# One trunk layer in fp32: the out-gate projection by seven block products, 23 weights split by adding transfers, and the gate's steps chained

## The chip, the cores and the metric

The kernel runs on one core of a Trainium2 chip. The metric is the device time of one execution in microseconds (us), as the median of the runs shown; lower is better. A profile is one execution recorded by the hardware profiler. Five engines work side by side, each with a queue of its own: TensorE (PE: matrix products into PSUM banks of 128 partitions x 512 fp32), VectorE (DVE), ScalarE (ACT), GpSimd (POOL) and SyncE (SP), which here only issues transfers. A transfer issued by POOL can add to what its destination holds; one issued by SP copies.

## The reference: what is computed

Input x is 512 tokens by 1024 channels, one layer, fp32 throughout.

```python
u = rmsnorm(x, norm1_g)
a_glu, q, k, v, r, g_low, gate_a, gate_b = split(u @ w_in)
# branch A: convolution module
c = a_glu[:, :1024] * sigmoid(a_glu[:, 1024:])
c = silu(layernorm(causal_depthwise_conv(c, width 31)))      # over 1024 channels
y_conv = c @ w_conv_out
# branch B: gated linear attention, 4 heads, dk 128, dv 256, chunks of 64
gk = log_sigmoid(g_low @ w_gate_up + b_gate) / 16
o = gla_chunked(q, k, v, gk)
o = rmsnorm_per_head(o) * gla_norm_g * silu(r)               # r: the out-gate, 512 x 1024
y_gla = o @ w_gla_out
h = x + (sigmoid(gate_a) * y_conv + sigmoid(gate_b) * y_gla) @ w_o
u2 = rmsnorm(h, norm2_g)
z = causal_depthwise_conv(u2 @ w_ffn_up, width 3)            # 5632 channels
h = h + (silu(z[:, :2816]) * z[:, 2816:]) @ w_ffn_down
out = rmsnorm(h, final_g)
```

## The kernel before, in words

**Products.** An fp32 product is made of three TensorE products (`mm3`, L294): both operands are split into a high part, rounded to the type TensorE takes at full speed (fp32r), and a low part, what is left. Low x high, high x low and high x high are added up in one PSUM bank. Lines L301, L302 and L303 are the three.

**Weights.** All weights come in blocks of 128 x 1024, in the order of one list, `order` (L149). `load` (L171) issues the transfer of the next block on SP into one of four `raw` buffers; `split_weight` (L229) makes the high part with an ACT copy (L240, L256) and the low part with a DVE subtraction (L241, L259), each into one of four buffers. `weight(name, j)` (L269) gives the block that is due and keeps the splitting two blocks ahead (`LOOK`). It also calls `fill(RATE)`: 5.0 units of waiting side work are taken from `chains` and issued behind the newest low part. The side work is the 31 taps of the width-31 convolution for each of eight channel tiles (`conv_tap`, L600, one DVE instruction each, L607) and, when all these are done, the LayerNorm of branch A in pieces (`norm_chain`, L688). So DVE's side work is spread over TensorE's time by counting weights.

A 128-column tile of a projection (`col_tile`, L305) is eight k-blocks times three products, 24 matmuls of 128x512.

**Stages in order of time.**
1. Start (to 34 us): x is loaded, transposed by TensorE and normalised; the order of the work is written out by hand. `spread_gain` (L382) turns the transposed token tiles 2 and 3 into high (L389, ACT) and low parts (L391, DVE) in pieces of 128x128; the first half of v is projected at the same time (L529).
2. `w_glu`: 16 column tiles, two for each channel tile of branch A; the sigmoid on ACT, the product on DVE (L615), then the 31 taps are put into `chains`.
3. `w_low`, the low-rank decay; its three steps Abs, Exp and Ln over four heads (`gate`, L724) are put on ACT in one piece, with the first block of the second half of v behind it (`values(1, gate)`, L742).
4. Heads (`Head`, L763; loop L884): for head h, TensorE projects q and k, then two column tiles of w_r (`gate_r`, L871: the tile of r and a Silu on ACT, L876), and the scores, states and outputs of head h − 1 are laid between them. `outputs` (L843) normalises with a root made on POOL (`rsqrt`, L347, L349) and multiplies on ACT (L859); `gated` (L861) transposes back on TensorE (L865), multiplies with gain and gate on DVE (L868) and splits.
5. `w_gb` and `w_gla` mixed (L880 to L916), with sigmoid(gate_b); then `w_ga` (L918) with its sigmoids. Meanwhile the LayerNorm runs as side work: mean on TensorE (L652), centred tiles (L655), squares (L657, L662), variance (L637), root, spread over the partitions (L644), and for each channel tile a product (L674), Silu (L676) and split (L684, L685).
6. `w_conv` with the merge, then w_o and, in three groups, the channel mixer with `w_up` and `w_down`.

**Seven block products.** `w_o` and `w_down` are already computed by a scheme in which a product of 2 x 2 blocks takes seven block products, not eight (`seven`, L958). The operands are the blocks named in `STEPS` (L48): a11 and a12 and a22 as they are, and s1, n2, s4 and n3 sums of blocks. The sums of weights are made in memory: a block is loaded into a `kept` tile, and a POOL transfer that adds brings the next one (L210, L227); DVE adds once (L220). A `block` (L185) takes one row of the weight's layout, which holds two k-blocks by 512 columns.

ACT can hold one set of function tables at a time; going from one set to another shows as a line ACT_TABLE_LOAD.

Of the kernel before, what the change touches and what calls it, by code (L numbers as in the profile page):

```python
# [17 lines left out]
P = 128  # L18
# [18 lines left out]
RATE = 5.0  # L37
WARM = 7
# [4 lines left out]
SEVEN = {"w_o": KT // 2, "w_down": FT // 2}  # L43
# [3 lines left out]
STEPS += [(step, d) for step in ("n2", "s4", "n3", "a22") for d in (0, 1)]  # L47
# [3 lines left out]

C_A, C_G, C_Q, C_K, C_V, C_R = 0, 1024, 2048, 2560, 3072, 4096
# [15 lines left out]
def trunk_layer(ctx: ExitStack, tc: tile.TileContext, a: dict, out: bass.AP):  # L68
# [16 lines left out]
    ps = pool("psum", 1, bass.MemoryType.PSUM)  # L85
    edge = ctx.enter_context(tc.tile_pool(name="edge", bufs=1, side="right"))
    heap_scope, hp = scoped("heap", 26)
    conv_scope, vp = scoped("conv", 10)
    gla_scope, gp = scoped("gla", 1, "right")

# [61 lines left out]
    order += [("w_v", KT // 2 + j) for j in range(KT // 2)]  # L152
    for h in range(HEADS):
        order += [("w_qk", 2 * h), ("w_qk", 2 * h + 1), ("w_r", 2 * h), ("w_r", 2 * h + 1)]
    order += [("w_gb", m) for m in range(AHEAD)]
    for m in range(KT):
        order += [("w_gla", m)] + [("w_gb", m + AHEAD)] * (m + AHEAD < KT)
# [25 lines left out]
    def block(name, pairs, d, row, col):  # L183

        pairs = pairs[2 * d : 2 * d + 2]  # L185
        first = pairs[0][row]
        w = a[name][col * SEVEN[name] + first // 2]
        return w if len(pairs) == 2 else w[:, row * T : (row + 1) * T]

    def keep_tile(name):  # L190
        if name == "w_o":
            return tp.tile([P, D], F32, tag="x", name=nm("kept"), bufs=3)
        return fp.tile([P, D], F32, tag="kept", name=nm("kept"), bufs=2)
# [3 lines left out]
    def load_block(name, pairs, step, d):  # L197
# [11 lines left out]
        if step == "n3":  # L209
            nc.gpsimd.dma_start(dst, block(name, pairs, d, 1, 1), accum_op=ALU.add)  # L210
# [4 lines left out]
    def operand(raw, pairs, step, d):  # L215
# [3 lines left out]
        if step == "n2":  # L219
# [3 lines left out]
    def sum_on(name, pairs, step, d):  # L223

        if step in ("a11", "n2"):
            nxt = block(name, pairs, d, *((0, 1) if step == "a11" else (1, 0)))
            nc.gpsimd.dma_start(kept[pairs, d], nxt, accum_op=ALU.add)  # L227

    def split_weight(between=None):  # L229
        if len(ready) < len(order):  # L230
# [4 lines left out]
            if name in SEVEN:  # L235
                raw = operand(raw, *spec)
# [4 lines left out]
                nc.vector.tensor_tensor(lo, raw, hi.bitcast(F32), ALU.subtract)  # L241
# [14 lines left out]
            nc.scalar.copy(hi, raw)  # L256
            if between:
# [10 lines left out]
    def weight(name, j, ahead=LOOK):  # L268
# [4 lines left out]
        fill(RATE)  # L273
# [215 lines left out]

    def renormed(t):  # L490
# [3 lines left out]
        for g in range(2):  # L494
            f = unscaled[t, g]
            nc.vector.tensor_tensor(by_token(f), by_token(f), rb, ALU.mult)
        for g in range(2):
            f = unscaled[t, g]
            split_by(by_token(f), *(u1[g][i][:, :, t * P : (t + 1) * P] for i in range(2)))
# [43 lines left out]
    here = lambda t: (lambda g, k: tuple(u1[g][i][:, k, t * P : (t + 1) * P] for i in range(2)))  # L543
# [25 lines left out]
    spread_gain(banks[2], 0, here(2))  # L569
# [5 lines left out]
    spread_gain(banks[3], 0, here(3))  # L575
# [13 lines left out]
    def values(n, middle):  # L589
        row_half("w_v", n * KT // 2, n, acts1, KT, v_done, n == 1, middle)  # L590

# [4 lines left out]

    conv = [None] * KT

# [9 lines left out]

    for k in range(KT):
        pg = col_tile(weight("w_glu", 2 * k + 1), acts1)  # L610
# [6 lines left out]
            [(1 if tap < CW - 1 else 0, lambda k=k, tap=tap, c=c: conv_tap(k, tap, c)) for tap in reversed(range(CW))]  # L617
        )


    ca = [None] * KT
    stat = {}

    def add_up(tiles, key):
        def first():
            stat[key] = btmp()
            nc.vector.tensor_tensor(stat[key], tiles(0), tiles(1), ALU.add)

        def more(k):
            nc.vector.tensor_tensor(stat[key], stat[key], tiles(k), ALU.add)  # L630

        return [first] + [lambda k=k: more(k) for k in range(2, KT)]
# [91 lines left out]
    def gate(step):  # L724
        if step > 0:
            return
        with tc.manual_schedule(engines={ET.Activation}):
            for h in range(HEADS):
# [4 lines left out]
                nc.scalar.activation(ab[h], pg, AF.Abs, bias=bg)  # L733
                ls.append(heap())
                nc.vector.tensor_scalar(ls[h], pg, bg, 0.0, ALU.add, ALU.min)
            for h in range(HEADS):
                nc.scalar.activation(ab[h], ab[h], AF.Exp, scale=-1.0)
            for h in range(HEADS):
                nc.scalar.activation(ab[h], ab[h], AF.Ln, bias=1.0)
                nc.vector.tensor_tensor(ls[h], ls[h], ab[h], ALU.subtract)  # L740

    values(1, gate)  # L742


# [17 lines left out]
    class Head:  # L762
# [11 lines left out]
        def decays(self):  # L774
# [8 lines left out]
            nc.scalar.activation(self.end, self.end, AF.Exp, scale=G16)  # L783
# [56 lines left out]
        def outputs(self):  # L840
            self.o = tp.tile([P, NT, DV], F32, tag="x", name=nm("o"), bufs=3)
            for g in range(2):
# [14 lines left out]
                for i in range(2):  # L857
                    o = self.o[:, 2 * g + i, :]
                    nc.scalar.activation(o, po[:, i * DV : (i + 1) * DV], AF.Copy, scale=r[:, i : i + 1])  # L859

        def gated(self):  # L861
            for s in range(2):
# [3 lines left out]
                f = tmp()  # L866
                m = 2 * self.h + s
                nc.vector.scalar_tensor_tensor(f, po, pp[:, PP_GG + s : PP_GG + s + 1], sr[m], ALU.mult, ALU.mult)  # L868
                oa[m] = split(f)

    sr = [None] * KT  # L871

    def gate_r(m):
# [4 lines left out]
    gbs = {}  # L878

    def gate_b(m):  # L880
        gbs[m] = col_tile(weight("w_gb", m), acts1)


# [419 lines left out]
```

## Time and profile before

| | |
|---|---|
| Time, median of 3 runs | 838.59 us (837.83 to 838.66) |
| The profiled execution | 838.75 us |
| Its span, first to last instruction | 837.0 us |
| Granted TensorE clock, mean | 0.997 |
| PE busy | 827.7 us, 99% of the span |
| PE's weight loads (beside the matmuls) | 691.3 us, 83% |
| DVE busy | 648.8 us, 78% |
| ACT busy | 400.0 us, 48% |
| POOL busy | 41.7 us, 5% |
| Bytes moved | 97.27 MB, 116 GB/s on average |

Busy shares are means over stages with different limits. A stage is read from the windows, which give each engine's busy time in a stretch, and from the waits, which say what TensorE stood still for and how long. In the chain of work that ended last, each piece is followed back to what released it; a piece is given with its start, its length and the line. In timelines, "x8" at the end of a row joins eight like instructions, and a bracket gives the idle time ahead of the row and who ended it. The mean duration of one matmul overlaps with that of the next, so the price of a matmul is taken from a row of many.

### The profile page before, as it was taken

What the parts mean: (1) busy time and instruction counts of PE and PEld (TensorE: products, weight loads), DVE (VectorE), ACT (ScalarE), POOL (GpSimd) and SP (SyncE); (2) the same over time, 40 slices, a digit from 0 to 9 for tenths busy, and PEclk for the clock granted to TensorE, in tenths of its full rate; (3) what the DMA queues carried; (4) which work ended last, traced back from release to release, by engine and by line L of the source; (5) the groups of instructions that cost most, each with busy time, mean ns of one, the idle gap of its engine ahead of it and who ended that gap; (6) DMA issues with size and microseconds to landing.
All of it is one profiled execution on the core that took longest, in us unless ns stands there. A gap on an engine that the chain in (4) does not pass through costs nothing.

```text
span 837.0 us, 10108 instructions
## 1 busy us (share of the span) xinstructions
PE 827.7 (99%) x3841; PEld 691.3 (83%) x3841; DVE 648.8 (78%) x952; ACT 400.0 (48%) x598; POOL 41.7 (5%) x64
## 2 busy tenths in 40 slices
PE   9999999999999999999999999999999999999996
PEld 7888888888888888888888898888888888888885
DVE  5789879999998798744687758778757787667795
ACT  7732337435443422449444765444434444444454
POOL 1000000000100100000001000001000010000111
PEclk9999999999999999999999999999999999999998
DMA  8332222222222322222347643234742249222462
GB/s 299 115 101 101 100 92 93 93 85 84 93 76 76 126 100 94 83 99 78 106 96 197 181 152 131 97 95 108 213 151 87 66 89 286 101 82 96 101 125 101
DMA packets 28465, 97.27 MB, mean 116 GB/s; under 512 B 3232, under 2 KB 3504, under 8 KB 28416
## 3 DMA queue, kind: packets, MB, share of 16 engines
q1 hardware_dynamic: 24784, 84.62, 29.8%
q0 software_dynamic: 3456, 11.80, 8.3%
q8 instruction: 30, 0.49, 0.2%
q10 hardware_dynamic: 176, 0.20, 0.1%
q14 instruction: 19, 0.16, 0.1%
HBM read 94.51 MB, written 2.10 MB: 115 GB/s over the span
## 4 chain that ended last, share of the span: by engine, by line
PE 90%; issue 3%; DVE 2%; DMA 2%; ACT 2%; POOL 0%; SPq 0%; POOLq 0%; ACTq 0%; DVEq 0%
PE mm L301 27%; PE mm L303 27%; PE mm L302 27%; PE mm L529 3%; DMA raw<-in_w_down_dram 1%; PE ax L848 1%; DVE hres L998 1%; DMA x<-in_x_dram 1%; PE ax L850 1%; PE ax L830 1%; PE ax L301 1%; PE ax L303 1%; PE ax L302 1%; PE ax L380 1%; ACT whi L240 0%
## 5 line engine op out<-in xcount | busy, mean ns | idle before, releaser
L301 PE MATMUL mm<-uh,wlo 128*128 128x512 f32 (+1 forms) x768 | 294.7, 384 | 0.0
L303 PE MATMUL mm<-uh,whi 128*128 128x512 f32 (+1 forms) x768 | 292.2, 380 | 0.0
L302 PE MATMUL mm<-ul,whi 128*128 128x512 f32 (+1 forms) x768 | 292.0, 380 | 0.0
L256 ACT CAST whi<-raw 128x1024 fp32r<-128x1024 f32 x116 | 120.9, 1047 | 126.3 <-PE mm L303 94.8
L259 DVE TENSOR_TENSOR wlo<-raw,whi 128x1024 fp32r<-128x1024 f32 x116 | 141.1, 1220 | 35.0 <-ACT whi L256 34.8
L303 PEld LDWEIGHTS mm<-uh,whi 128*128 128x128 f32 x768 | 144.4, 188 | 27.9
L302 PEld LDWEIGHTS mm<-ul,whi 128*128 128x128 f32 x768 | 144.5, 188 | 27.2
L301 PEld LDWEIGHTS mm<-uh,wlo 128*128 128x128 f32 x768 | 144.5, 188 | 27.0
L607 DVE SCALAR_TENSOR_TENSOR c<-h,pp,c 128x511 f32<-128x511 f32 (+14 forms) x240 | 162.6, 732 | 0.7
L1078 DVE SCALAR_TENSOR_TENSOR tmp<-mm,pp,tmp 128x511 f32<-128x511 f32 x88 | 65.8, 748 | 66.7 <-ACT tmp L1076 65.5
L1076 ACT ACTIVATE tmp<-mm,pp 128x512 f32<-128x512 f32 x44 | 34.3, 779 | 61.5 <-PE mm L303 61.5
L240 ACT CAST whi<-kept 128x1024 fp32r<-128x1024 f32 (+1 forms) x32 | 31.7, 994 | 25.1 <-DVE kept L220 11.3
L241 DVE TENSOR_TENSOR wlo<-kept,whi 128x1024 fp32r<-128x1024 f32 (+1 forms) x32 | 36.7, 1153 | 4.3 <-ACT whi L240 4.1
L998 DVE TENSOR_TENSOR hres<-hres,mm 128x512 f32<-128x512 f32 (+1 forms) x49 | 32.6, 671 | 6.1 <-PE mm L303 3.7
L240 ACT CAST whi<-raw 128x1024 fp32r<-128x1024 f32 (+1 forms) x24 | 23.7, 995 | 18.0 <-PE mm L303 16.8
L241 DVE TENSOR_TENSOR wlo<-raw,whi 128x1024 fp32r<-128x1024 f32 (+1 forms) x24 | 27.3, 1153 | 1.9 <-ACT whi L240 1.8
L302 PE MATMUL mm<-wlo,sh 128*128 128x512 f32 x66 | 25.8, 391 | 0.0
L303 PE MATMUL mm<-whi,sh 128*128 128x512 f32 x66 | 25.7, 389 | 0.0
L301 PE MATMUL mm<-whi,sl 128*128 128x512 f32 x66 | 25.5, 389 | 0.0
L301 PE MATMUL mm<-h,wlo 128*128 128x512 f32 x64 | 25.4, 397 | 0.0
L349 POOL TENSOR_TENSOR rstd<-var,mhalf 128x1 f32<-128x1 f32 (+1 forms) x16 | 13.3, 839 | 239.9 <-DVE var L855 196.6
L303 PE MATMUL mm<-h,whi 128*128 128x512 f32 x64 | 24.9, 390 | 0.0
(258 smaller groups left out, 1146.6 us busy)
## 6 DMA issues: line engine op xcount, KB each, us to landing
raw<-in_w_up_dram SPq DMA_DIRECT2D x44, 512.0 KB, 3.5
raw<-in_w_glu_dram SPq DMA_DIRECT2D x16, 512.0 KB, 3.3
raw<-in_w_down_dram SPq DMA_DIRECT2D x15, 512.0 KB, 3.3
kept<-in_w_down_dram POOLq DMA_DIRECT2D x10, 512.0 KB, 5.5
raw<-in_w_v_dram SPq DMA_DIRECT2D x8, 512.0 KB, 3.9
raw<-in_w_qk_dram SPq DMA_DIRECT2D x8, 512.0 KB, 3.2
raw<-in_w_r_dram SPq DMA_DIRECT2D x8, 512.0 KB, 3.3
raw<-in_w_gb_dram SPq DMA_DIRECT2D x8, 512.0 KB, 3.2
```

Source lines behind the costliest of these rows:

```text
L240: nc.scalar.copy(hi, raw)
L241: nc.vector.tensor_tensor(lo, raw, hi.bitcast(F32), ALU.subtract)
L256: nc.scalar.copy(hi, raw)
L259: pace[0] = nc.vector.tensor_tensor(lo, raw, hi.bitcast(F32), ALU.subtract)
L301: nc.tensor.matmul(acc, ll, rh, start=first, stop=False, **kw)
L302: nc.tensor.matmul(acc, lh, rl, start=False, stop=False, **kw)
L303: nc.tensor.matmul(acc, lh, rh, start=False, stop=last, **kw)
L529: nc.tensor.matmul(accs[t], src(k)[a_low], w, start=first, stop=last)
L607: nc.vector.scalar_tensor_tensor(y[:, s:], c[:, : T - s], w, y[:, s:], ALU.mult, ALU.add)
L998: nc.vector.tensor_tensor(hres[t, n][:, c], hres[t, n][:, c], x[:, c], op)
L1076: nc.scalar.activation(z, acc, AF.Identity, bias=pp[:, PP_FB + m : PP_FB + m + 1], scale=w[2])
L1078: nc.vector.scalar_tensor_tensor(z[:, s:], acc[:, : T - s], w[j], z[:, s:], ALU.mult, ALU.add)
```

## The change

**w_r by seven products.** r = u @ w_r moves out of the head loop. A `unit` computes it in the seven-product scheme, straight after the decay projection, with 14 weight blocks of 12 matmuls (`R_STEPS`). Its result lies by token instead of by channel: eight tiles `sr[t, n]` of 128 tokens x 512 columns. For this:
- w_r is laid out anew in DRAM, by 16 transfers on SP (`lay_rows`, two before each channel tile of w_glu), each 256 KB in pieces of 512 bytes, into eight tiles `rows_r`.
- All sums of w_r's blocks are made by adding transfers on POOL (eight of them); DVE adds none.
- The sums of activations (s1, n2, s4, n3) are formed on DVE and split on ACT and DVE, as a chain of side work. They need the activations as whole fp32 tiles, so the start keeps them (`whole`): for token tiles 2 and 3 `gained_normed` multiplies a 128x512 tile on DVE, then splits it with an ACT copy and a DVE subtraction, in place of `spread_gain`.

**23 low parts by transfers.** For the blocks in `ADDED` (seven of w_glu, all eight of w_gb and of w_gla) the low part is no longer subtracted on DVE: ACT writes the block's negative, rounded like the high part, and a POOL transfer adds the block once more from DRAM.

**Rates.** `fill` gets a rate of its own for each weight (`RATES`); the sums for the LayerNorm's mean are put into the chains of taps; the pauses in `norm_chain` are changed.

**Gate steps and Silus.** Abs, Exp and Ln are laid at three places of the r unit, and each ACT instruction is issued behind the one before (`behind`). The eight Silus of r run together, in place, after the decays of head 0. ACT_TABLE_LOAD goes from 22 to 13.

**Heads.** The places of w_r's tiles are taken by the second half of v (heads 0 and 1) and by w_gb's first four tiles (heads 2 and 3); the other four follow, then all of w_gla. The output's norm factor and the gate are multiplied in one DVE instruction (128x256) in place of ACT's; the gain is applied on the way back from the transposes, where ACT makes the high part and DVE the low.

The diff, cut to its core:

```diff
+RATES = {"w_glu": 6.2, "w_r": 0.3, "w_low": 0.0, "w_v": 5.0, "w_qk": 4.2, "w_gb": 6.0, "w_gla": 6.5, "w_ga": 9.0}
+ADDED = {("w_glu", 2 * k) for k in range(1, KT)} | {(name, m) for name in ("w_gb", "w_gla") for m in range(KT)}
-SEVEN = {"w_o": KT // 2, "w_down": FT // 2}
+SEVEN = {"w_o": KT // 2, "w_down": FT // 2, "w_r": KT // 2}
+R_STEPS = [("a11", 0), ("a11", 1), ("a12", 0), ("s1", 0), ("s1", 1), ("a12", 1)] + LATE
+GATE_AT = [("a11", 1), ("a12", 0), ("n2", 1)]
+    def lay_rows(j):
+        n, k = j // 4, j % 4 * 2
+        for i in range(2):
+            src = a["w_r"][n * 4 : n * 4 + 4, :, (k + i) * P : (k + i + 1) * P]
+            dst = rows_r[j][:, i * T : (i + 1) * T]
+            nc.sync.dma_start(dst.rearrange("p (c x) -> p c x", x=P), src.rearrange("c p x -> p c x"))
...
-    order += [("w_v", KT // 2 + j) for j in range(KT // 2)]
+    order += [("w_r", (O_PAIRS, step, d)) for step, d in R_STEPS]
...
+            if order[len(ready)] in ADDED:
+                nc.scalar.activation(lo, raw, AF.Copy, scale=-1.0)
+                nc.gpsimd.dma_start(lo, a[name][spec], accum_op=ALU.add)
+                ready.append((hi, lo))
+                load()
+                return
...
-        fill(RATE)
+        fill(RATES.get(name, RATE))
...
+    def gained_normed(t):
+        for g in range(2):
+            gain = gains[:, g * 4 : g * 4 + 4].unsqueeze(2).to_broadcast([P, 4, P])
+            nc.vector.tensor_tensor(into_whole(t, g)[0], by_token(banks[t][g]), gain, ALU.mult)
+        for g in range(2):
+            f, parts = into_whole(t, g)
+            split_by(f, *parts)
...
-    spread_gain(banks[2], 0, here(2))
+    gained_normed(2)
...
+    def sums_chain():
+        chain = []
+        for g in range(2):
+            chain += [(1, lambda n=n, g=g: form(n, g)) for n in ("s1", "n2", "s4", "n3")]
+        for n in ("s1", "n2", "s4", "n3"):
+            chain += [(1, lambda n=n, g=g: place(n, g)) for g in range(2)]
+        return chain
...
     for k in range(KT):
+        lay_rows(k)
         pg = col_tile(weight("w_glu", 2 * k + 1), acts1)
...
-        chain = [(1, f) for f in add_up(lambda k: conv[k], "sum")]
-        chain[-1] = (RATE, chain[-1][1])
-        chain.append((0, ln_mean))
+        chain = [(8, lambda: None), (0, ln_mean)]
         chain.extend((2, lambda k=k: ln_center(k)) for k in range(KT))
-        chain[-1] = (RATE, chain[-1][1])
-        chain.append((RATE, ln_var))
+        chain[-1] = (13, chain[-1][1])
+        chain.append((13, ln_var))
...
+    def behind(emit):
+        if last_act[0] is None:
+            last_act[0] = emit()
+            return
+        with tc.issue_after(last_act[0].ins):
+            last_act[0] = emit()
...
+        while steps:                       # unit("w_r", ...)
+            step, d = steps.pop(0)
+            parts = [(d, weight(name, (O_PAIRS, step, d)))]
...
+                        mm3(acc, (ah, al), (w[0][:, c], w[1][:, c]), opens and d == 0 and j == 0, last, not opens)
+                if parts[-1][0] == 1:
+                    at(step, i)
+                    sink(step, i, acc)
...
-                    nc.scalar.activation(o, po[:, i * DV : (i + 1) * DV], AF.Copy, scale=r[:, i : i + 1])
+                    nc.vector.scalar_tensor_tensor(self.o[:, t, :], half, r[:, i : i + 1], gate, ALU.mult, ALU.mult)
...
-                nc.vector.scalar_tensor_tensor(f, po, pp[:, PP_GG + s : PP_GG + s + 1], sr[m], ALU.mult, ALU.mult)
-                oa[m] = split(f)
+                nc.scalar.activation(hi, po, AF.Copy, scale=gain)
+                nc.vector.scalar_tensor_tensor(lo, po, gain, hi.bitcast(F32), ALU.mult, ALU.subtract)
...
-        pr = col_tile(weight("w_r", m), acts1)
-        sr[m] = heap()
-        nc.scalar.activation(sr[m], pr, AF.Silu)
+            if h == 0:
+                for y in sr.values():
+                    behind(lambda: nc.scalar.activation(y, y, AF.Silu))
```

More of the change, by code (lines that the diff above doesn't have):

```diff
@@ L541, in v_done @@
             nc.scalar.activation(vt[t, n], acc, AF.Copy, scale=r)
-    here = lambda t: (lambda g, k: tuple(u1[g][i][:, k, t * P : (t + 1) * P] for i in range(2)))
+    for half in range(2):
+        for g in range(2):
+            whole[half, g] = sum_tile()
     banks[1] = [ax_bank(), mm_bank()]
@@ L574, in trunk_layer @@
     r1[1] = rms(1)
-    spread_gain(banks[3], 0, here(3))
+    gained_normed(3)
     renormed(0)
@@ L617, in trunk_layer @@
             [(1 if tap < CW - 1 else 0, lambda k=k, tap=tap, c=c: conv_tap(k, tap, c)) for tap in reversed(range(CW))]
+            + [(1 if k else 0, lambda k=k: add_up(k))]
         )
     ca = [None] * KT
[L622 to L632, printed above, removed]
     def token_sums(s):
```

207 lines of the change are left out of this document (158 added, 49 removed).

## The prediction

> **What bounds the kernel now.** I read the page first (engine shares, then the engine shares of the chain that ended last), then the waits of TensorE, then the stages one by one.
>
> ```profile
> span 837.0 us, 10108 instructions
> PE 827.7 (99%) x3841; PEld 691.3 (83%) x3841; DVE 648.8 (78%) x952; ACT 400.0 (48%) x598; POOL 41.7 (5%) x64
> ...
> PE 90%; issue 3%; DVE 2%; DMA 2%; ACT 2%; POOL 0%; SPq 0%; POOLq 0%; ACTq 0%; DVEq 0%
> ```
>
> The waits of TensorE (us in total, times, longest), and one piece of the chain (start, us, what):
>
> ```profile
> PE ax L441 <- DVE ones L408: 1.1, 1, 1.1
> PE ax L380 <- DMA x<-in_x_dram: 0.7, 1, 0.7
> PE ax L380 <- ACT un L400: 0.3, 1, 0.3
> ...
> 28.74 5.49 PE mm L529 x24
> ```
>
> Stages (stretch, its length, busy time of PE, weight load, DVE, ACT and POOL, granted clock, DMA share, GB/s), the GLU projections, the heads, w_gla, w_ga and the output projection w_o:
>
> ```profile
> 34.00:121.40 87.40, 87.40 (x388) 72.35 (x387) 71.61 (x99) 28.48 (x35) 0.53 (x1) 1.00 0.35 117
> ...
> 147.00:276.00 129.00, 129.00 (x625) 108.76 (x624) 123.58 (x199) 57.12 (x95) 5.77 (x6) 1.00 0.26 86
> ...
> 293.00:358.00 65.00, 65.00 (x287) 53.45 (x286) 53.85 (x74) 19.73 (x26) 0.00 (x0) 1.00 0.29 97
> 358.00:401.00 43.00, 43.00 (x199) 35.84 (x198) 18.43 (x24) 32.73 (x40) 1.01 (x1) 1.00 0.24 80
> ...
> 444.00:490.00 46.00, 45.72 (x241) 38.87 (x240) 35.36 (x58) 30.03 (x58) 5.73 (x7) 1.00 0.72 213
> ```
>
> TensorE works in 99% of the span, and the chain is 90% TensorE. The three wait rows are all that the profile charges to it: 2.1 us. In each stage TensorE is full. So time falls only where matmuls go, and the other engines count only where they make TensorE wait. The narrow place is the heads: DVE 123.58 of 129 us. The profiled execution took 838.75 us, 0.16 above the median of 838.59; the sum is made against 838.75.
>
> **Matmuls removed.** Eight column tiles of 24 matmuls (192) become 14 weight blocks of 12 (168). The chain row prices 24 full matmuls at 5.49 us: **−5.5 us**. Every other matmul of the changed program is there in the same number. As TensorE had almost no waits to lose, this is also the most that can be won; all else can only take back.
>
> **Start.** For token tiles 2 and 3 the normalised activations were made in eight short pairs, ACT then DVE. Now DVE multiplies whole 512-wide tiles, ACT copies, DVE subtracts.
>
> ```profile
> 20.94 2.16 DVE L391 SCALAR_TENSOR_TENSOR ul<-ax,gains,uh 128x128 fp32r<-128x128 f32 x8 [0.32 <-ACT uh L389]
> ...
> 22.54 0.48 PE L529 MATMUL mm<-whi,ul 128*128 128x512 f32 x1
> ...
> 24.36 2.16 DVE L391 SCALAR_TENSOR_TENSOR ul<-ax,gains,uh 128x128 fp32r<-128x128 f32 x8 [0.87 <-ACT uh L389]
> ...
> 25.51 0.47 PE L529 MATMUL mm<-whi,ul 128*128 128x512 f32 x1
> ...
> 27.15 1.22 ACT L469 CAST uh<-h 128x512 fp32r<-128x512 f32 x2 [1.79 <-DVE h L496]
> ...
> 27.81 1.29 DVE L470 TENSOR_TENSOR ul<-h,uh 128x512 fp32r<-128x512 f32 x2
> ```
>
> The pairs gave a first low part soon after 20.94, and TensorE took it at 22.54. In the new form, from about 20.6: multiply 0.65, copy 0.61, subtract 0.65 (half of the last two rows) puts the first at 22.5 to 22.7, so a stall of up to 0.2. For tile 3, whose banks are read once DVE is done with tile 2 (about 23.4), two multiplies, the copy behind the first and a subtract end near 26.1, against 25.51: 0.6. I take **+0.8**, bounds 0 and 1.5 (all six steps of a tile in series, less the slack seen).
>
> **GLU stage.** Rate 6.2 in place of 5.0 means 2.4 more convolution taps per pair of weights; seven low parts leave DVE.
>
> ```profile
> L256 ACT CAST whi<-raw 128x1024 fp32r<-128x1024 f32 x116 | 120.9, 1047 | 126.3 <-PE mm L303 94.8
> L259 DVE TENSOR_TENSOR wlo<-raw,whi 128x1024 fp32r<-128x1024 f32 x116 | 141.1, 1220 | 35.0 <-ACT whi L256 34.8
> ...
> L607 DVE SCALAR_TENSOR_TENSOR c<-h,pp,c 128x511 f32<-128x511 f32 (+14 forms) x240 | 162.6, 732 | 0.7
> ...
> L227 POOL DMA_DIRECT2D kept<-in_w_down_dram x12: 849/862/878, 560.9 to 808.6; - x12
> ...
> DMA to landing us min/median/max: 3.9/5.5/9.2
> ...
> q1 hardware_dynamic: 24784, 84.62, 29.8%
> q0 software_dynamic: 3456, 11.80, 8.3%
> ```
>
> DVE per pair (11.0 us of TensorE): 12.4 taps at 0.73, one low part 1.22, one product 0.69, in all 11.0; two neighbours overlap a little (1.29 for two of 0.69, the last row of the fence before), so it is some 10.2: full, not over. Taps that come late delay nobody here. **0**, up to +1.
>
> **The 23 adding transfers.** Each replaces a 1.22 us subtraction by an ACT copy of the negative (1.05), a POOL issue (0.86) and a landing of 3.9 to 9.2 us: 7.4 median, 11.1 worst. A low part's buffer is free once the weight four places earlier is used, so three weights of 5.49 us (16.5) lie between. Covered, **0**. If the cover went (an ACT or POOL queue late by over 5 us), each late one would cost what is over. With the r unit's eight sums POOL issues 31 more, 27 us in all; they stand ahead of the small powers of the norms, at 0.86 us each.
>
> **Re-laying w_r.** 16 transfers of 256 KB, DRAM to DRAM in 512-byte pieces, go on SP, the queue of the weight loads; eight issue back to back ahead of one of the GLU loads. No row shows this kind. From the queue rows: SP moves 84.62 MB in 29.8% of 837 us, 339 GB/s, so 0.8 us a transfer if bytes set the price, 1.5 us at the adding queue's 170 GB/s, and, if a piece costs what a packet does (29.8% × 837 × 16 engines / 24784 = 161 ns), 512 × 161 / 16 = 5.2 us, 41 us for eight. SP may run about 15 us for eight of them before the load behind is late (three weights less one landing of 3 us): 60 ns a piece. I take the bytes' price, by the row of SP's own queue, which is the nearest: **0**; upper end +25. DRAM to DRAM both reads and writes; twice 0.8 is still under the 60 ns a piece (1.9 us).
>
> **The r unit.** 38 us of TensorE, like w_o, whose window shows 45.72 of 46 busy with the same steps. On the path: sums of weights that land by adding transfers.
>
> ```profile
> kept<-in_w_o_dram POOLq DMA_DIRECT2D x4, 512.0 KB, 7.0
> ```
>
> Ten loads at 1.29 us (161 ns × 128 / 16) and eight adds at 2.58 (8.3% × 837 × 16 / 3456 = 322 ns) are 33.5 us of 38: 88% DMA, more than w_o's 72%. The second s1 sum is needed some 5.5 us after its add can start; the add took 5.5 elsewhere and 7.0 in w_o. The 28 us of DVE (14 low parts, 16 sums and splits, sinks) fit. The chained gate steps wait on one another on ACT, with copies of weights behind them, but 27 us of ACT fit in 38. **+0.5**; bounds 0 and 3.7 (9.2 − 5.5).
>
> **Heads.** The gate multiply moves into the normalisation, on DVE. Two groups of the heads' window (count, then busy us, mean ns, then idle before):
>
> ```profile
> L868 DVE SCALAR_TENSOR_TENSOR tmp<-ax,pp,h 128x512 f32<-128x512 f32 x6 | 4.2, 746 | 1.5 <-PE ax L865 1.5
> ...
> L837 DVE SCALAR_TENSOR_TENSOR state<-state,dec,ax 128x256 f32<-128x256 f32 x8 | 3.8, 476 | 0.0
> ```
>
> Per head DVE gains four 128x256 products (4 × 0.476 = 1.9) and changes two products and two subtractions (2 × 0.746 + 2 × 0.69) for two products (1.5): +0.5. Taps go from 20 to 18.4 in heads 0 and 1 (−1.2) and to 20.4 in heads 2 and 3 (+0.3), where two low parts go too (−2.4). DVE so ends at 27.4 and 26.5 us of a 29.3 us head, against 28.1 before. But its products now lie between the norm and the transposes that TensorE is to do next, and four late value banks (then four gb banks) hold four of five `mm` banks. **+0.2**; bounds 0 and 2 (0.5 a head).
>
> **w_gla, w_ga, LayerNorm.** w_gla loses eight subtractions in a stage where DVE has 11 us to spare. The LayerNorm is set closer:
>
> ```profile
> 341.06 0.86 PE ax L652 x2
> ...
> 357.26 0.69 DVE L662 TENSOR_TENSOR btmp<-btmp,btmp 128x512 f32<-128x512 f32 x1 [0.76 <-ACT btmp L657]
> ...
> 363.72 0.79 PE ax L637 x8
> ...
> 370.11 0.89 PE ax L644 x8
> ...
> 371.81 1.28 ACT L676 ACT_TABLE_LOAD   x1
> 373.10 1.52 ACT L676 ACTIVATE btmp<-c,pp 128x512 f32<-128x512 f32 x2
> ```
>
> Between mean (341.06) and variance (363.72) lie four weights now, three (16.5 us) after; the squares were done 16.9 after the mean, so up to 0.6 is lost, less as some DVE work between them is gone. From the spread (370.11) to the convolution's projection lay 28 us; now 16.5, and the first two column tiles are interleaved, so that the last normalised tile is wanted some 9.5 us later: 26. ACT's work there, eight Silus, eight copies, four table loads and the weights' copies, is some 21 to 25 us. **+0.3**; bounds 0 and 1.5. Table loads go from 22 to 13 (−11.5 us of ACT), mostly where ACT has idle time: 0.
>
> **Sum:** 838.75 − 5.5 + 0.8 + 0.5 + 0.2 + 0.3 = 835.05, or **834.9** as a median.
>
> **Rivals.**
> *A, no change.* The sums of the r unit or the heads' norm come late at several of these steps: 3.7 (r) with 1.5 (start) and the LayerNorm's 0.6 gives 5.8 back: about 838.5. For it: DMA 88%, adds at 7.0. Against: w_o lost 0.28.
> *B, slower: the re-laying starves the weight loads.* It decides from about 85 ns a piece (8 × 512 × 85 / 16 = 21.8 us, some 7 more than the cover); at 100 ns the loss is 10.6 and the time 845.5. For it: eight in a row ahead of a load, and 161 ns for a packet of 3.4 KB. Against: 512-byte pieces carry a seventh of those bytes.
> *C, slower: DVE in the heads.* DVE was at 96%; if its new products wait on the norm's power behind POOL issues, each head loses 2 us or so: 8 us, 843. Against: 0.7 to 1.6 us a head freed.
> *D, table loads cost more than their row.* With an extra stop of 1.4 us at each of the four loads of the LayerNorm's last part, that chain grows by 5.5 to some 29 of its 26: about +4, 839. Against it: the row at 371.81 ends at 373.09 and the next instruction starts at 373.10.
>
> The Trainium skill (ScalarE: Activation LUTs, What ACT_TABLE_LOAD costs) has that stop: 1283 ns of load and about 1380 ns of drain, 2.66 us a switch. This trace shows the load and no drain, so D gets little.
>
> **Chances.** Forecast 0.60 (832.9 to 836.9); A 0.14; B 0.12; C 0.09; D 0.03; 0.02 is left for more gain than the sum. The measurement tells apart 0.2%, 1.7 us: same is 836.9 to 840.3. Faster 0.62; same 0.15 (A with part of D); slower 0.23. The range leaves out little below 833 (nothing but −5.5 pays) and half of B above: 833.0 to 843.0; the forecast's own is 833.0 to 836.9.
>
> **What would show it.** TensorE with 24 fewer 128x512 matmuls and 819 to 823 us busy; waits in the start on the tile split of under 1.5 us; in the r unit waits on weights under 2 us together; no wait on a GLU weight while the re-laying runs; heads of 29.3 us with DVE under 96%; the convolution's projection not waiting over 1 us. The forecast is wrong if a `w_glu` load lands late behind the re-laying, if adds in the r unit land after 9 us, or if a head is longer than 30 us.

## The result

The changed kernel takes 835.61 us (median of 7 runs, 834.5 to 836.71), the kernel before 838.41 in the same session (7 runs, 837.83 to 838.66). The ratio is 0.9967, with a 95% interval of 0.9955 to 0.9978: 2.8 us faster. Forecast were 834.9 us and a range of 833.0 to 843.0. In two further sessions the same kernel had medians of 835.46 and 835.46, at ratios of 0.9959 (0.9948 to 0.9971) and 0.9965 (0.9952 to 0.9977).

The page of the changed kernel, its first two lines, and three of the wait rows of TensorE (us in total, times, longest):

```profile
span 834.2 us, 10185 instructions
...
PE 823.8 (99%) x3817; PEld 686.7 (82%) x3817; DVE 645.3 (77%) x957; ACT 415.9 (50%) x606; POOL 69.6 (8%) x95
```

```profile
PE ax L411 <- DVE ul L422: 1.2, 1, 1.2
...
PE ax L332 <- DVE h L818: 0.6, 1, 0.6
...
PE mm L581 <- DVE ul L501: 0.2, 1, 0.2
```

TensorE has 24 instructions fewer, and the span is 2.8 us shorter (837.0 before). 24 matmuls are 5.45 us at the 0.227 us from one start to the next that both traces have, so part of it came back. The three rows name the largest pieces: 0.2 in the start, 0.6 in the r unit, and 1.2 in the norm behind w_o, a stage that the change doesn't touch. A row counts idle time alone. All that TensorE lost is got by taking each distance from one start to the next over the median of its kind, adding these up, and taking off the same sum of the trace of before: 0.6 us in the start, 0.8 in the r unit, 0.2 to 0.3 in the heads, 0.3 in the LayerNorm and 1.3 in w_o's stage. As x landed 0.1 us earlier, this makes 3.15 us in all.

That is 0.5 us more than the spans leave room for. The rest lies behind the last matmul, from the issue of the last SP transfer of the output (before, then changed) to the end of the span:

```profile
832.59 0.33 SPq L1160 DMA_DIRECT2D out_dram<-y  x1
```

```profile
830.29 0.33 SPq L1322 DMA_DIRECT2D out_dram<-y  x1
```

It took 4.4 us before (to 837.0) and 3.9 after (to 834.2). Outside the span it is the other way: time less span is 2.0 us in the changed kernel's runs and 1.7 in those of before, so that 0.2 us of the shorter end reach the time. With these the profiled execution adds up: 838.75 − 5.45 + 3.15 − 0.2 = 836.25, and it took 836.23. Why the end differs isn't shown.

The stages of the changed kernel (length, busy time of PE, weight load, DVE, ACT, POOL, clock, DMA share, GB/s): GLU, r unit, heads with the rest of w_gb's first tiles, w_o.

```profile
34.00:121.90 87.90, 87.90 (x390) 72.78 (x389) 79.78 (x118) 39.08 (x51) 7.66 (x9) 1.00 0.63 165
...
125.40:163.50 38.10, 37.55 (x166) 30.73 (x165) 29.15 (x34) 27.52 (x37) 5.27 (x7) 1.00 0.79 192
163.50:293.00 129.50, 129.50 (x627) 109.19 (x626) 122.09 (x208) 61.32 (x97) 15.48 (x16) 1.00 0.48 122
...
441.00:487.00 46.00, 44.54 (x232) 37.73 (x231) 34.89 (x57) 29.45 (x56) 5.73 (x7) 1.00 0.72 208
```

TensorE is full in the GLU stage and in the heads, where DVE is at 91% and 94%. It loses 0.55 us in the r unit and 1.46 in w_o's stage.

**The start.** The first matmul that takes token tile 3, and DVE ahead of it:

```profile
25.98 0.50 PE L581 MATMUL mm<-whi,ul 128*128 128x512 f32 x1 [0.17 <-DVE ul L501]
```

```profile
23.78 0.16 DVE L488 SCALAR_TENSOR_TENSOR var<-ss 128x1 f32<-128x1 f32 x1 [0.68 <-ACT junk L486]
23.86 1.28 DVE L548 TENSOR_TENSOR f<-ax,gains 128x512 f32<-128x512 f32 x2
25.23 1.29 DVE L501 TENSOR_TENSOR ul<-f,uh 128x512 fp32r<-128x512 f32 x2
```

It starts at 25.98, 0.47 later than before. DVE stood 0.68 us for the sum of a norm that ACT had not squared yet (L488), and only then made tile 3's products.

**The r unit.** Five rows, of ACT, DVE and TensorE, in the order in which each stands behind the one above:

```profile
130.09 1.05 ACT L265 CAST whi<-kept 128x1024 fp32r<-128x1024 f32 x1 [1.37 <-DMA kept<-rows]
131.04 1.04 ACT L265 CAST whi<-raw 128x1024 fp32r<-128x1024 f32 x1
```

```profile
132.96 1.22 DVE L266 TENSOR_TENSOR wlo<-raw,whi 128x1024 fp32r<-128x1024 f32 x1
134.21 2.07 DVE L818 TENSOR_SCALAR h<-ax,pp 128x512 f32<-128x512 f32 x3
```

```profile
135.02 0.50 PE L332 MATMUL ax<-whi,ul 128*128 128x512 f32 x1 [0.55 <-DVE h L818]
```

ACT waits 1.37 us for an adding transfer (which took 5.4 us to land, no more than such a transfer mostly does), DVE makes low parts behind ACT, the gate's minimum (L818) stands behind these low parts, and its PSUM bank is the one that the step a12 wants.

**w_o.** Part of the chain of work that ended last (start, us, what):

```profile
453.42 0.60 POOL kept L252
454.02 13.53 DMA kept<-in_w_o_dram
...
467.65 1.06 ACT whi L265
...
468.74 1.23 DVE wlo L266
469.96 0.08 DVE var L1203
```

One adding transfer of w_o took 13.5 us to land; the slowest of the kernel before was 9.2. The norm's variance (L1203) stands on DVE behind the low part of that sum, and TensorE's transposes (L411) wait for what is made from it.

**Re-laying and adding.** The two lines of the re-laying transfers, and the landing times of the 23 adding ones:

```profile
L99 SPq DMA_DIRECT2D rows<-in_w_r_dram x16: 552/677/2523, 7.9 to 28.1; - x16
...
DMA to landing us min/median/max: 4.4/6.3/8.0
```

```profile
DMA to landing us min/median/max: 5.3/6.9/10.0
```

All 16 were issued between 7.9 and 28.1 us. Eight of them stand back to back ahead of a GLU load:

```profile
20.07 8.76 SPq L99 DMA_DIRECT2D rows<-in_w_r_dram  x8
33.43 4.16 SPq L191 DMA_DIRECT2D raw<-in_w_glu_dram  x4
```

They are issued by 28.8 us, and that load goes out at 33.43, where the kernel before issued it at 33.19. No wait of TensorE is charged to either kind.

### The profile page after: what moved, and what is told of

The parts are those of the page before. It is cut to its first block, busy times and chain, and to the rows that moved or that the text cites. A ratio compares the mean times of both kernels' runs of the same rounds, so it can differ in the third digit from the quotient of the medians.

```text
span 834.2 us, 10185 instructions
## 1 busy us (share of the span) xinstructions
PE 823.8 (99%) x3817; PEld 686.7 (82%) x3817; DVE 645.3 (77%) x957; ACT 415.9 (50%) x606; POOL 69.6 (8%) x95
## 4 chain that ended last, share of the span: by engine, by line
PE 86%; DMA 4%; issue 4%; ACT 2%; DVE 2%; POOL 1%; SPq 0%; POOLq 0%; ACTq 0%; DVEq 0%
PE mm L332 26%; PE mm L333 26%; PE mm L334 26%; DMA kept<-in_w_o_dram 2%; PE mm L581 1%; PE ax L332 1%; PE ax L999 1%; PE ax L333 1%; PE ax L334 1%; DMA x<-in_x_dram 1%; DMA kept<-rows 1%; DMA raw<-in_w_o_dram 1%; PE ax L1001 1%; PE ax L981 1%; DMA hres<-in_x_dram 1%
## 5 line engine op out<-in xcount | busy, mean ns | idle before, releaser
L332 PE MATMUL mm<-uh,wlo 128*128 128x512 f32 (+1 forms) x704 | 269.8, 383 | 0.0
L334 PE MATMUL mm<-uh,whi 128*128 128x512 f32 (+1 forms) x704 | 267.3, 380 | 0.0
L333 PE MATMUL mm<-ul,whi 128*128 128x512 f32 (+1 forms) x704 | 267.1, 379 | 0.0
L688 DVE SCALAR_TENSOR_TENSOR c<-h,pp,c 128x507 f32<-128x507 f32 (+21 forms) x240 | 162.3, 732 | 1.2 <-ACT c L685 0.6
L333 PEld LDWEIGHTS mm<-ul,whi 128*128 128x128 f32 x704 | 132.5, 188 | 25.0 <-ACT h L1082 0.2
L332 PEld LDWEIGHTS mm<-uh,wlo 128*128 128x128 f32 x704 | 132.5, 188 | 24.9 <-issue 0.2
L334 PEld LDWEIGHTS mm<-uh,whi 128*128 128x128 f32 x704 | 132.4, 188 | 25.0
L290 DVE TENSOR_TENSOR wlo<-raw,whi 128x1024 fp32r<-128x1024 f32 x85 | 103.2, 1220 | 14.7 <-ACT whi L281 14.4
L283 ACT ACTIVATE wlo<-raw 128x1024 fp32r<-128x1024 f32 x23 | 24.4, 1061 | 74.0 <-PE mm L332 68.5
L252 POOL DMA_DIRECT2D kept<-in_w_down_dram x12 | 10.3, 859 | 271.8 <-DVE wlo L266 271.8
```

Source lines behind the costliest of these rows:

```text
L283: nc.scalar.activation(lo, raw, AF.Copy, scale=-1.0)
L290: pace[0] = nc.vector.tensor_tensor(lo, raw, hi.bitcast(F32), ALU.subtract)
L332: nc.tensor.matmul(acc, ll, rh, start=first, stop=False, **kw)
L333: nc.tensor.matmul(acc, lh, rl, start=False, stop=False, **kw)
L334: nc.tensor.matmul(acc, lh, rh, start=False, stop=last, **kw)
L688: nc.vector.scalar_tensor_tensor(y[:, s:], c[:, : T - s], w, y[:, s:], ALU.mult, ALU.add)
```

## Experiments

Each ratio is to the kernel before in the same session, since that had medians from 838.4 to 840.5 in the several sessions. In the session of experiments 1 to 4 it took 840.49, and the changed kernel as it is was not run there. The ratios of these four don't stand beside its 0.9959 to 0.9967, and the waits in the traces decide. All but one are edits of the changed kernel.

**1. Leave out 24 matmuls.**

```diff
-                for d, w in parts:
+                for d, w in parts if step != "a22" else ():
```

> The changed kernel without the 24 matmuls of the r unit's last step (a22); its weights are still loaded and split. It leaves out one of the seven block products, so part of r is missing. Theory (TensorE sets the pace of the r unit, and 24 matmuls are worth 24 x 0.227 = 5.45 us wherever they are taken): 835.6 - 5.5 = 830.1, between 829 and 831.5, and the stretch of the r unit 32.7 us long in place of 38.1. Rival (the adding transfers or DVE set the pace there, so that the sums come late once the matmuls are shorter): less than 3 us gained, 832.6 or more, with waits of TensorE on weights behind the unit.

831.38 us against 840.49 before: 0.9892 (0.9878 to 0.9907). Experiments 3 and 4 took 834.8 and 834.9 us in the same session, so some 3.5 us more; the span is 828.4 us against 833.3 in experiment 5's first profile, 4.9 us less. The r unit's stretch:

```profile
125.40:158.10 32.70, 32.30 (x142) 26.39 (x141) 24.50 (x28) 25.28 (x34) 5.25 (x6) 1.00 0.86 209
```

```profile
PE mm L332 <- DVE q L945: 0.7, 1, 0.7
```

TensorE is busy for 32.30 of 32.70 us with DMA at 86%; a new wait of 0.7 us comes in the first head. The theory holds: the time lies in its range, TensorE sets the pace of the unit, and by the spans 24 matmuls are worth their 5.45 us less the new wait. What the change lost was not lost by a unit bound by its sums.

**2. Subtract again, with no adding transfers for the 23 weights.**

```diff
-ADDED = {("w_glu", 2 * k) for k in range(1, KT)} | {(name, m) for name in ("w_gb", "w_gla") for m in range(KT)}
+ADDED = set()
```

> The changed kernel with all 23 low parts made by DVE subtractions again, no adding transfer for them; rates and all else as changed. Theory (the adding transfers pay for the higher rates): DVE gets 7 x 1.14 = 8.0 us more in the GLU stage, 79.8 + 8.0 = 87.8 of 87.9 us, and 8 x 1.14 = 9.1 us more from the heads to the end of w_gb, 122.1 + 9.1 = 131.2 of 129.5 us: over-full, so TensorE waits there for low parts, 2 to 5 us in all, 837.5 to 840.5. Rival (DVE has slack enough, since its order can let taps slip): the same time as the changed kernel, 835.6 within 0.8.

836.14 us, 0.9948 (0.9931 to 0.9965). The theory fell, since the waits that it named are absent; the rival's figure came. It is still 1.3 us above experiments 3 and 4 of the same session.

```profile
34.00:121.90 87.90, 87.90 (x389) 72.86 (x388) 86.33 (x124) 33.26 (x43) 0.53 (x1) 1.00 0.34 122
...
163.50:293.00 129.50, 129.50 (x628) 109.36 (x627) 120.90 (x198) 52.48 (x87) 7.15 (x6) 1.00 0.24 85
```

```profile
PE ax L332 <- DVE h L818: 1.1, 1, 1.1
```

DVE is at 98% in the GLU stage and TensorE still never waits there. The heads have not more DVE work but less (120.90): side work slips to later stages, where there is room. The adding transfers save DVE 25 us (670.1 us busy without them, 645.3 with) and TensorE, by this profile, only part of the 1.1 us at the gate: in the r unit it lost 2.4 us here, against 0.8 in the changed kernel's first profile.

**3. The swap in the start.**

```diff
-    r1[1] = rms(1)
     gained_normed(3)
+    r1[1] = rms(1)
```

> The changed kernel with one swap in the start: the products and splits of token tile 3 are put ahead of the norm of tile 1 (its two squares on ACT, its sum on DVE). Theory (the stall of 0.47 us at 25.5 us comes of tile 3's first low part, which stands on DVE behind that sum): the first matmul of tile 3 starts at 25.5 in place of 25.98 and 0.3 to 0.5 us go: 835.2. Rival (the two products, the copy and the subtraction alone are too long): the stall stays at 0.3 or more, 835.6. Rival (the norm of tile 1 now comes late for the next tile): a new stall near 28.9.

834.82 us, 0.9933 (0.9919 to 0.9948).

```profile
23.13 1.28 DVE L548 TENSOR_TENSOR f<-ax,gains 128x512 f32<-128x512 f32 x2
24.50 1.29 DVE L501 TENSOR_TENSOR ul<-f,uh 128x512 fp32r<-128x512 f32 x2
```

The products start at 23.13, and no wait on L501 is left; the next tile isn't late. The profile settles it, since 0.4 us is less than the spread of the times. The theory holds: not the longer chain itself but its place on DVE, behind the norm of another tile, made the stall.

**4. PSUM banks changed over.**

```diff
-bank[of[step], i] = ax_bank() if step == "a12" else mm_bank()
+bank[of[step], i] = ax_bank() if step == "s1" else mm_bank()
```

> The changed kernel with the PSUM banks of two steps of the r unit changed over: a12 takes banks of the kind mm, s1 takes banks of the kind ax. Theory (TensorE's wait of 0.6 us at 134.1 is for the banks of the gate's products, which DVE reads late): the wait goes, 0.5 to 0.8 us less, 834.9, and no wait is charged to the gate's minimum on DVE. Rival (the wait is moved on to the step s1, or was hidden by another): 835.6.

834.86 us, 0.9935 (0.992 to 0.9949), but the wait is there:

```profile
PE ax L332 <- DVE h L818: 0.4, 1, 0.4
```

It has moved to the step s1, which now wants these banks. That was the first rival; the time alone would have spoken for the theory.

**5. The changed kernel again, twice.**

> The changed kernel as it is, so that it stands beside the other runs on one chip. Theory (the stall of 1.2 us at 475 us in its first profile, behind an adding transfer of w_o that took 13.5 us to land, is one execution's and no part of the change): that wait is absent, or under 0.3 us, and the span is 833 to 833.5. Rival (the change has moved the transfers of w_o's stage, which it does not touch, so that the add lands late as a rule): the wait at 470 to 476 us is there again with 1 us or more.

835.46 us (835.41 to 835.65), span 833.3 us. No wait in w_o's norm beyond that of the kernel before: the theory held for the wait. But an add of w_o took 12.1 us to land here too, so the slow landing is not one execution's. In place of that wait another shows in the r unit, with the chain behind it:

```profile
132.31 9.97 DMA kept<-rows
...
142.38 1.06 ACT whi L265
...
143.46 1.24 DVE wlo L266
...
144.74 0.50 PE mm L333
```

The add of a weight sum (POOL, on `kept`) took 9.97 us, and TensorE waits for the low part behind it, 0.3 us.

> The changed kernel as it is, once more beside the version with both small moves. Theory: 835 to 836 us, and of the waits of TensorE those at 25.5 us (0.3 to 0.4), at 134 us (0.3 to 0.7) and at 144 us (0.1 to 0.4) are there again, the one at 475 us, seen in one of the earlier profiles with 1.2 us, not or small.

835.46 us (834.16 to 836.69). The profiled execution was the shortest of the five, 834.16. The stall in the start is there again with 0.4 us and that at 134 us with 0.4, those at 144 and 475 us are not: in the r unit TensorE lost 0.5 us in all, and in w_o's stage no more than in the kernel before.

**6. The swap and an earlier gate.**

```diff
-    r1[1] = rms(1)
     gained_normed(3)
+    r1[1] = rms(1)
...
-GATE_AT = [("a11", 1), ("a12", 0), ("n2", 1)]
+GATE_AT = [("a11", 0), ("a12", 0), ("n2", 1)]
```

> The swap in the start (tile 3's products ahead of tile 1's norm) and the gate's first step one place earlier in the r unit (after the first of the two a11 tiles). Theory (what holds TensorE at 134 us is a chain: the adding transfer for the first s1 sum lands late, ACT waits for it, the low part on DVE waits for ACT, the gate's minimum stands behind that on DVE, and its bank is wanted by a12): the gate's products now come 2.7 us earlier, but the minimum still stands behind the same low part on DVE, so 0.2 to 0.6 us stay at 131 to 135 us; the start's 0.4 us go. Against the changed kernel in the same call: 0.3 to 0.9 us less. Rival (an earlier gate is enough): no wait over 0.1 us left there. Rival (the low-rank product isn't split yet at the earlier place): a new wait of 0.3 us or more at 128 us.

834.45 us (6 runs) against the changed kernel's 835.46 in the same session: 1.0 less, at 0.9954 (0.9941 to 0.9967). One of its runs took 837.28.

```profile
128.63 2.07 DVE L818 TENSOR_SCALAR h<-ax,pp 128x512 f32<-128x512 f32 x3
```

```profile
PE ax L813 <- DVE h L797: 0.2, 1, 0.2
```

The gate's minimum now runs at 128.63, ahead of the late low part, not behind it as expected, and the wait at 134 is gone: the first rival. The second came too: 0.4 us ahead of 127.4 until the low-rank product is split.

> The version with tile 3's products ahead of tile 1's norm and the gate's first step one place earlier, once more, since one of its six times was 2.5 us above the others. Theory: 0.8 to 1.2 us under the changed kernel in the same call, the sum of the waits that its first profile did not show. Rival (its gain was the chance of one profile): within 0.3 us of the changed kernel.

834.73 us (834.02 to 837.89) against 835.46: 0.7 less, between the theory's 0.8 and the rival's 0.3; 0.9957 (0.9944 to 0.9969). The profile fell on the longest run, 837.89, and shows what that is made of:

```profile
PE ax L411 <- DVE ul L422: 2.0, 1, 2.0
...
PE mm L333 <- DVE wlo L266: 0.8, 1, 0.8
```

Both are waits behind adding transfers, in w_o's norm and in the r unit, the first of them on the same path as the 1.2 us of the first profile. Against this version's first profile (834.17) the two stages lost 2.8 us more, of 3.8 us between the spans. The version was shorter by its median in both sessions, but the intervals overlap, so its gain over the changed kernel is not proved by times.

**7. The adding transfers alone, in the kernel before.** (The same two lines as in the change, put into the kernel before; the rate stays 5.0.)

> The kernel before with one part of the change alone: the 23 low parts made by ACT and adding transfers, with the old rate and everything else as it was. Theory (DVE is off the path, so relief for it buys nothing by itself, and the adding transfers are covered by 16 us of lead): ratio to before 1.000, between 0.9985 and 1.0015, with DVE 23 x 1.14 = 26 us less busy. Rival (the landings of 7 to 10 us make weights late): waits of TensorE on weights, 1 us or more slower. Rival (DVE at 96% in the heads cost something that no wait row shows): 1 us or more faster.

839.0 us against 838.69: 1.0005 (0.9997 to 1.0014).

```profile
PE 828.3 (99%) x3841; PEld 691.4 (83%) x3841; DVE 620.9 (74%) x929; ACT 421.2 (50%) x621; POOL 62.1 (7%) x87
```

DVE is 27.9 us less busy (648.8 before) and the time is the same. The theory holds, both ways: no weight came late, and relief for an engine off the path bought nothing. The one new wait of TensorE, 0.3 us at 291.5, is for a product of the last head, not for a weight.

**8. Lay w_r out twice.**

```diff
         lay_rows(k)
+        lay_rows(k, more_r)
```

> The changed kernel with w_r laid out twice, into a second set of DRAM tiles that nothing reads: 16 more transfers of 256 KB in pieces of 512 bytes on SP. Theory (a piece costs 27 ns, 0.86 us of all 16 engines for a transfer, and they run in the start behind x and the first weights, with slack): 13.8 us more of transfers move the time by 0 to 1 us. Rival (the start is at the limit of the DMA engines, 80 to 90% busy up to 40 us, so that the first GLU weights come late): 3 us or more, with TensorE waiting on weights between 30 and 60 us.

834.8 us, 0.9954 (0.9942 to 0.9967).

```profile
L100 SPq DMA_DIRECT2D rows<-in_w_r_dram x16: 552/692/1691, 7.5 to 50.2; - x16
L100 SPq DMA_DIRECT2D more<-in_w_r_dram x16: 557/694/4927, 10.0 to 55.9; - x16
```

The 32 transfers reach into the GLU stage, and TensorE has no wait between 30 and 60 us. Rival B of the prediction is out with room to spare.

**9. Gate steps and Silus not chained.**

```diff
-        if last_act[0] is None:
-            last_act[0] = emit()
-            return
-        with tc.issue_after(last_act[0].ins):
-            last_act[0] = emit()
+        emit()
```

> The changed kernel with the gate's ACT steps and the Silus of r no longer issued one behind the other; places as changed. The table loads go from 13 to 16. Theory (ACT has idle time where these loads lie, and a load costs its 1.28 us only): 3 x 1.28 = 3.8 us more of ACT, the time the same as the changed kernel within 0.8 us, 834.7 to 836.3. Rival (the chaining is what keeps ACT's copies of weights on time): TensorE waits on weights in the r unit or head 0, 1.5 us or more slower.

836.45 us (10 runs), 0.9967 (0.9957 to 0.9977); experiment 10, whose trace has the changed kernel's waits, had 835.04 in the same session.

```profile
160.43 0.47 PE L332 MATMUL mm<-whi,ul 128*128 128x512 f32 x1 [0.46 <-DVE h L865]
...
163.79 0.51 PE L332 MATMUL mm<-whi,ul 128*128 128x512 f32 x1 [0.40 <-DVE h L865]
```

```profile
156.85 0.63 ACT L1047 ACTIVATE h<-h 128x512 f32<-128x512 f32 x1 [1.06 <-DVE h L867]
157.39 1.04 ACT L265 CAST whi<-kept 128x1024 fp32r<-128x1024 f32 x1
```

Neither expectation fits: not a wait on weights, but two on PSUM banks that DVE reads late (L865, the unit's n3 step), 0.9 us in all. The rows of ACT show why: the Silus of r (L1047), no longer held back behind head 0's decays, have moved into the unit. There the later ones wait on ACT for DVE to finish their tiles (1.06 us here, 1.09 at 160.31), copies of weights stand behind it, DVE's low parts follow late, and n3's subtraction stands behind these. So it is the place of the Silus that the chaining keeps, rather than table loads. What it is worth is not settled: 1.4 us by the medians above and 0.9 by the waits, but the ratio of 0.9967 is also that of the changed kernel in its first session.

**10. Two more table loads in the LayerNorm's last part.**

```diff
         s = btmp()
+        if k == 6:
+            nc.scalar.activation(junk(P)[:, :1], n[:, :1], AF.Sigmoid)
         nc.scalar.activation(
```

> The changed kernel with one Sigmoid of a single column put ahead of the Silu of the seventh channel tile in the LayerNorm's last part: two more table loads, in the very stretch (394 to 402 us) where the convolution's projection waits for the last normalised tile. Theory (a load costs its row, 1.28 us, and nothing behind it; the chain is just on time, with 0.3 us of stall now): the last Silu and split move by 2 x 1.28 + 0.2 = 2.8 us, less what TensorE has in other work there, so a stall of 2 to 3 us at 397 to 402 and 1.7 to 2.7 us more in all. Rival D of the prediction (each load stops ACT for 1.4 us more): the chain moves by 5.5 us, 4.5 us or more in all. Rival (the chain has slack): no change.

835.04 us, 0.9951 (0.9938 to 0.9964): no change, which is the last rival's figure.

```profile
399.44 1.28 ACT L755 ACT_TABLE_LOAD   x1
400.73 0.21 ACT L755 ACTIVATE junk<-c 128x1 bf16<-128x1 f32 x1
400.84 0.60 ACT L764 CAST ch<-btmp 128x512 fp32r<-128x512 f32 x1
401.46 1.28 ACT L756 ACT_TABLE_LOAD   x1
402.76 1.52 ACT L756 ACTIVATE btmp<-c,pp 128x512 f32<-128x512 f32 x2
```

A load ends at 400.72, and the next instruction starts at 400.73; ahead of the second load ACT worked until 401.44. So the row is the whole price. The last split moved from about 402 to 406 us, and TensorE lost no more than in the changed kernel (0.2 us here). Its order there is another: the three profiles of the changed kernel have the same sequence of matmul lines, and this one differs. As I read the sequence, a third column tile is mixed in where the changed kernel had two, and its matmuls do not need the late tile; the planner that lays out the program seems to have reckoned with the two loads. So the run rules rival D out by its rows, but it doesn't show that the chain had slack, since the order moved along with the loads.

## Why the prediction was right

*Matmuls, −5.5.* Right: 24 matmuls at 0.227 us are 5.45, and experiment 1 takes 24 more out and shortens the span by 4.9 us, with a new wait of 0.7. It was the gain but for the 0.2 us at the program's end, which "all else can only take back" had not foreseen. TensorE's busy time fell to 823.8 us, just outside the 819 to 823 forecast.

*Start, +0.8.* The mechanism was right, the size 0.6. Tile 2's stall (0.2 forecast) came with about 0.1: its first matmul started at 22.55, before at 22.54, but the transposes ahead of it had started at 21.50 in place of 21.61. For tile 3 the end of the first subtraction was forecast near 26.1 and came at 25.9. What the working missed is why: of it 0.7 us was DVE's wait at L488, which a swap of two lines takes away.

*GLU stage, 0; adding transfers, 0.* Right. The landings were 5.3 to 10.0 us, inside the 16.5 us of lead. The GLU loads beside them landed after 6.5 us (median), 3.3 before and 3.3 in experiment 2, which has no such adds; that too was covered. That the adds "pay for" the higher rate was not the prediction's claim, but it was mine in experiment 2, and it fell.

*Re-laying, 0.* Right in value, place and price. Eight do run back to back ahead of a GLU load, as forecast, and in 8.8 us (20.07 to 28.8), of the 15 that were thought to be free. In the trace of the changed kernel the 8192 packets of 512 bytes took 27 ns each (median), so 0.86 us of the 16 engines for a transfer, where the price by bytes was 0.8; rival B's 85 ns and the upper end's 161 were far off.

*r unit, +0.5.* The mechanism was right, sums that come late; the term was mostly too small, and its path was not seen. The unit lost 0.8 us in the first profile, 1.3 and 0.5 in the two of experiment 5, and 2.2 in the run of 837.89 us in experiment 6. The forecast looked at the second s1 sum; the first wait goes by way of the gate's minimum on DVE and a PSUM bank. The bound of 3.7 us held. The prediction named adds of this unit that land after 9 us as a sign of being wrong. They came in the first profile already, with 9.1 and 10.2 us (10.0 in experiment 5's first, 11.9 in experiment 4), and did little harm; the sign was set too low. DMA was busy for 79% of the unit, where 88% had been worked out.

*Heads, +0.2; LayerNorm, +0.3.* Right: 0.2 to 0.3 each by the distances of matmuls against those of before. DVE ended at 122.09 of 129.5 us, 27.6 a head, where 27.4 and 26.5 were worked out. Rivals C and D are out: no head wait, and D's stop isn't there. Two figures of the rivals were off in themselves: A's 5.8 us taken back give 838.9 as a median, not 838.5, and D's chain of 29 in a room of 26 is 3 us late, not 4. Neither changes a rival's place.

The Trainium skill (ScalarE: Activation LUTs, What ACT_TABLE_LOAD costs) adds about 1380 ns of drain to a load. Experiment 10 shows 0.01 and 0.02 us from the end of its loads to the next instruction; the measurement decides.

*Table loads, 0.* Right as far as is shown: a load costs its row, and two more of them changed nothing in experiment 10. What the working missed is that the chaining which took some of them away also keeps the Silus from standing ahead of copies of weights, 0.9 us of waits in experiment 9.

*Not in the sum:* w_o's norm, 1.3 us in the first profile. The code there is the same. The terms that took back summed to 1.8; TensorE lost 3.15 us in the first profile, and 2.3 and 1.2 in the two of experiment 5, where w_o's wait was absent. So the mechanism of each term held, but that their sum came as near as it did is in part luck: the r unit alone swings by 0.8 us between these three executions, and w_o's norm was not reckoned with.

Why w_o's add lands late in some executions is shown in part. The wait was seen with 1.2, 2.0 and 0.5 us (the changed kernel, experiment 6's second run, experiment 8). In all three POOL issued w_o's last two adds without a gap behind a third (453.42 to 455.44 in the first). Four more profiles have the same row of issues. In these seven the last add landed after 10.8 to 13.9 us. In the five profiles with 0.9 us between the last two adds, and in the two of the kernel before and its variant, it landed after 9.1 to 10.1 us, with no such wait. Among the seven, only landings of 13.1, 13.5 and 13.9 us made TensorE wait; those of 10.8 to 12.1 did not. So the row of issues goes with the slow landing, and the stall is what exceeds some 12 to 13 us. Why POOL gets to issue them in a row in some executions, and what sets 10.8 or 13.9, is open; no run was made for it.

## What to carry to other kernels

When TensorE has 99% of the span, take the saving from the matmuls that go and look for the losses on the way of each new sum: transfer, copy, low part, whatever stands behind it on DVE, and the bank that this holds. A stall behind a longer chain can be one of order, as in the start, and a swap of two lines is cheaper than a shorter chain. Relief for an engine off the path is worth nothing until a stage is shown to wait for it.

## What the runs showed of the hardware

A packet of an adding transfer took 328 ns (median) in the first profile of the changed kernel, and one of a load of weights, with the same 4 KB, 159 ns. The landing of an adding transfer of 512 KB on `kept` took 3.9 to 13.5 us there, and up to 13.9 in the longest run of experiment 6; loads of weights on SP took 2.5 to 11.3, so the tail is not that of adds alone. That the adds widen the spread of a kernel's times isn't shown: the changed kernel's runs lie within 2.2 us in one session (834.5 to 836.71) and within 0.24 in another, where 17 runs of the kernel before spread over 1.9 (837.82 to 839.75). A re-laying from DRAM to DRAM in 512-byte pieces landed after 4.4 to 8.0 us for 256 KB, with 27 ns a piece. An ACT_TABLE_LOAD took 1.283 us in every trace, and where ACT had work at hand the next instruction started 0.01 to 0.02 us behind it.
